# A hybrid decoder block on one core: mean square from token-major x on ScalarE, the scan phases' low part on ScalarE, the scores' scale in the rotation tables, and the last quarter of the scan taken last in the GLU

## Chip, core and metric

One core of a Trainium2 chip. The metric is the time of one execution on the device in microseconds (us), as the median of several runs. Inputs and weights lie in HBM in float32.

## What is computed

The reference is one decoder layer on 256 tokens of width 1024. Cut to what matters here:

```python
h = rms_norm(x, norm_mix_g)                  # x * rsqrt(mean(x*x) + 1e-6) * g
q, k, v, u, g = split(h @ w_in)              # 1024, 1024, 1024, 512, 2048 columns
q, k = rotary(q), rotary(k)                  # cos and sin tables by position
o_a = softmax(causal(q @ k.T * 128**-0.5)) @ v   # 8 heads of 128; one block of 256 tokens
o_b = s5_branch(u, ...)                      # complex diagonal scan, then gelu, then a GLU:
                                             #   hgl = gelu(y) @ w_glu; val * sigmoid(gate)
x = x + (sigmoid(g_a) * o_a + sigmoid(g_b) * o_b) @ w_out
x = x + square(relu(rms_norm(x, norm_mlp_g) @ w_up)) @ w_down
out = rms_norm(x, norm_final_g)
```

In the scan each of the 2048 states turns by an angle per step; the kernel needs the cosine and sine of (angle x position) for 16 tiles of 128 states.

## The kernel before, in words

**Products in three passes.** Each float32 product is made of three matmuls on rounded halves: weight high x input high, weight high x input low, weight low x input high (`mm3`, and `tok_mm` with the roles changed, L266 to L268). The halves come from `split` (L83, L84): ScalarE (ACT) casts the raw tile to its high half `hi_*`, VectorE (DVE) subtracts to get the low half `lo_*`. The names `hi_v`, `lo_v`, `raw_v` stand for the weights of v, and so on for q, k, g (first gate), gb (second gate), glu, wo, up and dn. Raw weights come in tiles of 512 KB over the SP queue (L70) into five buffers; four buffers each hold the high and the low halves.

**Order.** The engines' orders are not written by hand. A scheduler with a timing model places every instruction; `tc.high_priority` moves some forward, and the string `ORDER` gives the sequence of the parts of the first half: V (two chunks of v), P and C (small operations that prepare the scan), T (angle tables), Q (a quarter of the scan), K (q and k of a pair of heads), G, S, A (gate, scores and output of a pair of heads), B (second gate), X (a change of the ACT table set), Y (gelu). Each engine then runs its own list strictly in order; all loads named here go through SP's queue in its order.

**The parts that the change touches.**
- The first matmuls, u_acc (L180), run while x arrives in transposed form (xT, four pieces). From the same pieces ACT squares (sq, L185 and L187), DVE adds the squares up (L188), and PE sums over channels with matmuls against ones into ms (L205). DVE makes rsm of it (L208); POOL and DVE compute its reciprocal root in `rsqrt` (L192 to L200, the multiplications on POOL); rs_half is half of it (L213), rs_ps (L216) turns it into a row for all partitions.
- v runs in eight units of 12 matmuls of 512 columns, units 0 to 3 for the first chunk; unit n needs raw_v_n, hi_v and lo_v.
- `tables(m)` makes four angle tables per call: ACT multiplies positions by the high part of the angle (L515, tile q), DVE takes off whole turns (L516, L517) and adds positions times the low part (L519, one call for each of four tiles, tile tha). ACT then takes absolute values and sines (cs, sn).
- `prepare` makes the small coefficients s (L376 to L388, 128x16 each), then the tiles Bs on DVE and POOL (L454, L462), which PE transposes into the tile bt (L470) and ACT copies to W2.
- `attn_head` takes row maxima of the scores, multiplies them by minus the scale (L315), and gives the scale to the two Exp calls.
- After the first half `gelu` makes the four quarters of the scan's output into yhl, and the GLU's four column blocks q run over k = 0 to 3, each followed by a merge with the gates.

Of the kernel before, what the change touches and what calls it, by code (L numbers as in the profile page):

```python
# [16 lines left out]
P = 128  # L17
D = 1024
# [27 lines left out]
         "B0 G3 S3 X1 Y0 A3 B1")  # L46


def build(ctx, tc, dr, out):
# [14 lines left out]
    def att_bank(name):  # L64
        return bank("att", 2, name)
# [72 lines left out]
    early = {0: w_load(dr["w_in"][0], "v00")}  # L138
    cst = keep.tile([P, 896], F32, name="cst")
# [3 lines left out]
    ones = keep.tile([P, 1], F32, name="ones")  # L143
    V.memset(ones, 1.0)
# [13 lines left out]
    sq = p1.tile([P, KD, T], F32, tag="yhl", name="sq")  # L158
# [25 lines left out]
    for i, xk in enumerate((x0, xT[:, 1, :])):  # L184
        S.activation(sq[:, i, :], xk, AF.Square)  # L185
    for c in range(1, 4):
        S.activation(sq[:, 2 * c : 2 * c + 2, :], xT[:, 2 * c : 2 * c + 2, :], AF.Square)  # L187
        V.tensor_add(sq[:, 0:2, :], sq[:, 0:2, :], sq[:, 2 * c : 2 * c + 2, :])  # L188
# [13 lines left out]
    ms = att_bank("ms")  # L202
    for h in range(2):
        for i in range(2):
            PE.matmul(ms[:, 0, h : h + 1], sq[:, i, h * P : (h + 1) * P], ones,  # L205
                      start=(i == 0), stop=(i == 1))
    rsm = p1.tile([P, 6], F32, name="rsm")
    V.tensor_scalar(rsm[:, 0:2], ms[:, 0, 0:2], 1.0 / D, EPS, op0=ALU.mult, op1=ALU.add)  # L208
# [25 lines left out]
    V.tensor_mul(rcos, cos_c, rs)  # L234
    V.tensor_mul(rsin, sin_c, rs)
# [34 lines left out]
    def flat(x):  # L270
        return x.rearrange("p a b -> p (a b)")
# [29 lines left out]
    scale = P ** -0.5  # L301
    mixA = p1.tile([P, KD, T], F32, name="mixA")

    def attn_head(q, k, j):
        s = att_bank("s").rearrange("p a b -> p (a b)")
        PE.matmul(s[:, 0:128], q[:, j, 0:128], k[:, j, 0:128], start=True, stop=False,
                  skip_group_check=True)
        PE.matmul(s[:, 0:128], ident_b, tri_b, start=False, stop=True, skip_group_check=True)
        PE.matmul(s[:, 128:384], q[:, j, 128:256], k[:, j, :], start=True, stop=False,
                  skip_group_check=True)  # L310
        PE.matmul(s[:, 256:384], ident_b, tri_b, start=False, stop=True, skip_group_check=True)
        st = p1.tile([P, 6], F32, tag="st", bufs=2, name="st")
        V.tensor_reduce(st[:, 0:1], s[:, 0:128], axis=mybir.AxisListType.X, op=ALU.max)
        V.tensor_reduce(st[:, 1:2], s[:, 128:384], axis=mybir.AxisListType.X, op=ALU.max)
        V.tensor_scalar(st[:, 0:2], st[:, 0:2], -scale, None, op0=ALU.mult)  # L315
        pr = p1.tile([P, 384], F32, tag="pr", bufs=2, name="pr")
        act(pr[:, 0:128], s[:, 0:128], AF.Exp, bias=st[:, 0:1], scale=scale,
                     accum_out=st[:, 2:3])
        act(pr[:, 128:384], s[:, 128:384], AF.Exp, bias=st[:, 1:2], scale=scale,
                     accum_out=st[:, 3:4])  # L320
        V.reciprocal(st[:, 4:6], st[:, 2:4])
        S.activation(pr[:, 0:128], pr[:, 0:128], AF.Copy, scale=st[:, 4:5])
        S.activation(pr[:, 128:384], pr[:, 128:384], AF.Copy, scale=st[:, 5:6])
        return pr
# [276 lines left out]
    for step in ORDER.split():  # L601
# [24 lines left out]
        elif part == "Y":  # L626
            gelu()
# [16 lines left out]
    for q in range(4):  # L644
        acc = wide_banks(f"glu{q}") if q % 2 else [flat(mm_bank(f"glu{q}{h}")) for h in range(2)]
        for kk_ in range(2):
            wh, wl = w_unit(dr["w_glu"][2 * q + kk_], f"glu{q}{kk_}")
            for k2 in range(2):
                k, w = 2 * kk_ + k2, slice(k2 * 512, (k2 + 1) * 512)
                for hf in range(2):  # L650
                    tok_mm(acc[hf], wh[:, w], wl[:, w], yhl[0][:, 0:4], yhl[0][:, 4:8], k, hf,
                           k == 0, k == 3)
# [12 lines left out]
        split(mxh[:, two, :], mxl[:, two, :], mixA[:, two, :])  # L665
    ph1.__exit__(None, None, None)
# [213 lines left out]
```

## Time and profile before

| | |
|---|---|
| median of 3 runs | 404.85 us (404.71 to 405.25) |
| the profiled execution, its own time | 405.1 us |
| its span, first to last instruction | 403.2 us |
| PE busy / DVE busy / ACT busy | 98% / 73% / 56% |
| mean granted TensorE clock | 0.995 |
| DMA | 71.57 MB, mean 178 GB/s |

How to read it: all times below are us from the first instruction of the profiled execution. A row of the timeline has the start, the duration, the engine, the line of the program, the operation, output and input tiles with their shape, and a count where like instructions follow each other; in brackets is the time that the engine had stood idle before, and what ended it. Durations of neighbours on one engine overlap a little, so what an operation adds to its queue is the distance from start to start. Matmuls overlap most: a matmul of 256 columns shows 0.28 us and the next one starts 0.12 us later.

### The profile page before, as it was taken

Reading aid. Unit: us, or ns where it says so; the run is one execution under the profiler, and the core shown is the slowest. Engines: PE = TensorE matmul, PEld = TensorE weight load, DVE = VectorE, ACT = ScalarE, POOL = GpSimd, SP = SyncE. Lnnn points to the kernel's source line nnn. Section 1 sums busy time; section 2 is a strip of 40 time slices with the busy share of each in tenths; the row PEclk is TensorE's granted clock in tenths of the full one; section 3 lists DMA queues with packets and bytes.
Section 4 is the critical chain, followed back from the end, with each engine's and each line's share of the span. In section 5 each row is a group of like instructions: output and inputs, shape, how many; then the busy total and the mean of one; then the engine's idle time right before and its main releaser. Section 6 shows DMA issues by size and latency. Waiting matters only on the chain.

```text
span 403.2 us, 6862 instructions
## 1 busy us (share of the span) xinstructions
PE 394.3 (98%) x2635; PEld 355.2 (88%) x2635; DVE 292.8 (73%) x520; ACT 225.9 (56%) x360; POOL 30.3 (8%) x39
## 2 busy tenths in 40 slices
PE   8999999999999999999999999999999999999993
PEld 5988898989899787888889999999999888889983
DVE  5999999999999994769748665656565443564425
ACT  6767977655276557945647645464546334353323
POOL 4151492000000000000000000000000000000000
PEclk9999999999999999999999999999999999999998
DMA  8994843354516252456486465554555565555202
GB/s 228 401 337 149 246 154 102 111 202 151 192 56 208 84 195 102 158 159 206 161 308 209 152 215 191 176 194 172 191 178 193 172 205 169 199 192 178 101 0 104
DMA packets 23199, 71.57 MB, mean 178 GB/s; under 512 B 2944, under 2 KB 5248, under 8 KB 23168
## 3 DMA queue, kind: packets, MB, share of 16 engines
q1 hardware_dynamic: 20144, 68.92, 50.6%
q10 hardware_dynamic: 3024, 2.23, 1.9%
q8 instruction: 20, 0.33, 0.3%
q14 instruction: 11, 0.09, 0.1%
HBM read 69.18 MB, written 1.05 MB: 174 GB/s over the span
## 4 chain that ended last, share of the span: by engine, by line
PE 84%; DVE 5%; DMA 4%; ACT 2%; POOL 2%; issue 1%; ACTq 1%; SPq 0%; DVEq 0%
PE up L89 8%; PE up L90 8%; PE up L88 8%; PE dn L735 6%; PE dn L734 6%; PE dn L733 6%; PE k L88 2%; PE k L89 2%; PE k L90 2%; PE gb L268 2%; PE gb L266 2%; PE gb L267 2%; PE glu L268 2%; PE glu L266 2%; PE dnq L733 2%; PE dnq L735 2%
## 5 line engine op out<-in xcount | busy, mean ns | idle before, releaser
L89 PE MATMUL up<-x2l,hi_up 128*128 128x256 f32 x256 | 72.5, 284 | 0.0
L90 PE MATMUL up<-x2h,lo_up 128*128 128x256 f32 x256 | 72.3, 283 | 0.0
L88 PE MATMUL up<-x2h,hi_up 128*128 128x256 f32 x256 | 71.8, 283 | 0.0
L84 DVE TENSOR_TENSOR lo_dn<-raw_dn,hi_dn 128x1024 fp32r<-128x1024 f32 x32 | 39.2, 1225 | 44.0 <-ACT hi_dn L83 44.0
L83 ACT CAST hi_dn<-raw_dn 128x1024 fp32r<-128x1024 f32 x32 | 33.5, 1048 | 51.6 <-PE dn L735 25.8
L84 DVE TENSOR_TENSOR lo_up<-raw_up,hi_up 128x1024 fp32r<-128x1024 f32 x32 | 38.8, 1223 | 27.7 <-ACT hi_up L83 27.7
L83 ACT CAST hi_up<-raw_up 128x1024 fp32r<-128x1024 f32 x32 | 33.3, 1046 | 39.2 <-PE up L89 18.5
L89 PEld LDWEIGHTS up<-x2l,hi_up 128*128 128x128 f32 x256 | 49.1, 192 | 0.2 <-DVE x2l L694 0.2
L90 PEld LDWEIGHTS up<-x2h,lo_up 128*128 128x128 f32 x256 | 49.1, 192 | 0.0
L88 PEld LDWEIGHTS up<-x2h,hi_up 128*128 128x128 f32 x256 | 48.9, 192 | 0.1
L734 PE MATMUL dn<-lo_dn,hh 128*128 128x512 f32 x96 | 38.0, 395 | 0.0
L735 PE MATMUL dn<-hi_dn,hl 128*128 128x512 f32 x96 | 38.0, 395 | 0.0
L733 PE MATMUL dn<-hi_dn,hh 128*128 128x512 f32 x96 | 37.9, 395 | 0.0
L735 PEld LDWEIGHTS dn<-hi_dn,hl 128*128 128x128 f32 x96 | 18.0, 188 | 4.2
L733 PEld LDWEIGHTS dn<-hi_dn,hh 128*128 128x128 f32 x96 | 18.0, 188 | 3.8
L734 PEld LDWEIGHTS dn<-lo_dn,hh 128*128 128x128 f32 x96 | 18.0, 188 | 3.7
L89 PE MATMUL g<-xgl,hi_g 128*128 128x256 f32 x64 | 18.8, 294 | 0.0
L88 PE MATMUL k<-xgh,hi_k 128*128 128x256 f32 x64 | 18.4, 287 | 0.0
L90 PE MATMUL q<-xgh,lo_q 128*128 128x256 f32 x64 | 18.3, 286 | 0.0
L90 PE MATMUL g<-xgh,lo_g 128*128 128x256 f32 x64 | 18.3, 286 | 0.0
L90 PE MATMUL k<-xgh,lo_k 128*128 128x256 f32 x64 | 18.3, 286 | 0.0
L89 PE MATMUL q<-xgl,hi_q 128*128 128x256 f32 x64 | 18.3, 285 | 0.0
(267 smaller groups left out, 1046.9 us busy)
## 6 DMA issues: line engine op xcount, KB each, us to landing
raw_up<-w_up SPq DMA_DIRECT2D x32, 512.0 KB, 3.4
raw_dn<-w_down SPq DMA_DIRECT2D x32, 512.0 KB, 3.3
raw_v<-w_in SPq DMA_DIRECT2D x8, 512.0 KB, 6.0
raw_q<-w_in SPq DMA_DIRECT2D x8, 512.0 KB, 3.8
raw_k<-w_in SPq DMA_DIRECT2D x8, 512.0 KB, 3.2
raw_g<-w_in SPq DMA_DIRECT2D x8, 512.0 KB, 4.2
raw_gb<-w_in SPq DMA_DIRECT2D x8, 512.0 KB, 3.8
raw_glu<-w_glu SPq DMA_DIRECT2D x8, 512.0 KB, 3.2
```

The costliest lines, as they stand in the source:

```text
L83: ins = S.copy(hi, x).ins
L84: V.tensor_sub(lo, x, hi.bitcast(F32))
L88: PE.matmul(o, wh, xh, start=first, stop=False, **kw)
L89: PE.matmul(o, wh, xl, start=False, stop=False, **kw)
L90: PE.matmul(o, wl, xh, start=False, stop=last, **kw)
L266: PE.matmul(acc, xh[:, k, rows], wh, start=first, stop=False)
L267: PE.matmul(acc, xh[:, k, rows], wl, start=False, stop=False)
L268: PE.matmul(acc, xl[:, k, rows], wh, start=False, stop=last)
L733: PE.matmul(acc, xh, wh[:, w], start=(k == 0), stop=False, skip_group_check=True)
L734: PE.matmul(acc, xh, wl[:, w], start=False, stop=False, skip_group_check=True)
L735: PE.matmul(acc, xl, wh[:, w], start=False, stop=(k == 31), skip_group_check=True)
```

## The change

1. **Mean square.** x is loaded a second time, token-major, as one tile xtok of 1 MB, over SP directly behind the first tile of v's weights. Two ACT Squares of 1024 columns with an accumulated sum give ss; the squares of xT, the three DVE adds, ones and the ms matmuls are gone.
2. **Angle tables.** The four DVE operations of a call at L519 become four more ACT multiplications into a tile ulo and one DVE addition of 512 columns.
3. **Scale.** The rotation tables rcos and rsin carry the factor 128^-0.25 each, so scores come out scaled; the row maxima are negated where they are taken, and L315 is gone.
4. **GLU.** gelu is called for quarters 0 to 2 first. For q = 0 and 1 the GLU runs k = 0 to 2 of both, then comes gelu of quarter 3, the attention output of the last pair of heads (A3, taken out of `ORDER`), then k = 3 and the merge of each. q = 2 and 3 run as before.

```diff
-         "B0 G3 S3 X1 Y0 A3 B1")
+         "B0 G3 S3 X1 Y0 B1")
...
     early = {0: w_load(dr["w_in"][0], "v00")}
+    xtok = p1.tile([P, 2, D], F32, tag="yhl", name="xtok")
+    nc.sync.dma_start(xtok, dr["x"].rearrange("(h p) d -> p h d", p=P))
     cst = keep.tile([P, 896], F32, name="cst")
...
-    for i, xk in enumerate((x0, xT[:, 1, :])):
-        S.activation(sq[:, i, :], xk, AF.Square)
-    for c in range(1, 4):
-        S.activation(sq[:, 2 * c : 2 * c + 2, :], xT[:, 2 * c : 2 * c + 2, :], AF.Square)
-        V.tensor_add(sq[:, 0:2, :], sq[:, 0:2, :], sq[:, 2 * c : 2 * c + 2, :])
+    ss = p1.tile([P, 2], F32, name="ss")
+    for h in range(2):
+        S.activation(xtok[:, h, :], xtok[:, h, :], AF.Square, accum_out=ss[:, h : h + 1])
...
-    ms = att_bank("ms")
-    for h in range(2):
-        for i in range(2):
-            PE.matmul(ms[:, 0, h : h + 1], sq[:, i, h * P : (h + 1) * P], ones,
-                      start=(i == 0), stop=(i == 1))
     rsm = p1.tile([P, 6], F32, name="rsm")
-    V.tensor_scalar(rsm[:, 0:2], ms[:, 0, 0:2], 1.0 / D, EPS, op0=ALU.mult, op1=ALU.add)
+    V.tensor_scalar(rsm[:, 0:2], ss, 1.0 / D, EPS, op0=ALU.mult, op1=ALU.add)
...
-    V.tensor_mul(rcos, cos_c, rs)
-    V.tensor_mul(rsin, sin_c, rs)
+    V.scalar_tensor_tensor(rcos, cos_c, P ** -0.25, rs, op0=ALU.mult, op1=ALU.mult)
+    V.scalar_tensor_tensor(rsin, sin_c, P ** -0.25, rs, op0=ALU.mult, op1=ALU.mult)
...
-        V.tensor_reduce(st[:, 0:1], s[:, 0:128], axis=mybir.AxisListType.X, op=ALU.max)
-        V.tensor_scalar(st[:, 0:2], st[:, 0:2], -scale, None, op0=ALU.mult)
+        V.tensor_reduce(st[:, 0:1], s[:, 0:128], axis=mybir.AxisListType.X, op=ALU.max,
+                        negate=True)
-        act(pr[:, 0:128], s[:, 0:128], AF.Exp, bias=st[:, 0:1], scale=scale,
+        act(pr[:, 0:128], s[:, 0:128], AF.Exp, bias=st[:, 0:1],
...
+        ulo = rot("ulo")
         for q in range(4):
             S.activation(uhi[:, q, :], tpos, AF.Copy, scale=hi[:, 4 * m + q : 4 * m + q + 1])
+            S.activation(ulo[:, q, :], tpos, AF.Copy, scale=nlo[:, 4 * m + q : 4 * m + q + 1])
...
-        for q in range(4):
-            V.scalar_tensor_tensor(ang[:, q, :], tpos, nlo[:, 4 * m + q : 4 * m + q + 1],
-                                   ang[:, q, :], op0=ALU.mult, op1=ALU.add)
+        V.tensor_add(ang, ang, ulo)
...
+    first = [(q, glu_banks(q), glu_weights(q)) for q in range(2)]
+    for q, acc, ws in first:
+        glu_part(acc, ws, range(3))
+    gelu([3])
+    with tc.high_priority(ATT_PRIO):
+        attn_out(3, prs.pop(3), tha.pop(3))
+    for q, acc, ws in first:
+        glu_part(acc, ws, [3])
+        merge(q, acc)
+    for q in (2, 3):
+        acc = glu_banks(q)
+        glu_part(acc, glu_weights(q), range(4))
+        merge(q, acc)
```

`glu_part` holds the old inner loop for the given k, `merge` the old rest of the loop over q.

The change moves instructions at three places that the prediction speaks of. The rows are each engine's own order; the number behind a name is a buffer's.

The SP queue from the first tile of v's weights on, before:

```order
L70 DMA raw_v_87<-w_in 128x1024
L140 DMA cst<-cst 128x896
L70 DMA raw_v_328<-w_in 128x1024
L70 DMA raw_v_346<-w_in 128x1024
L70 DMA raw_v_364<-w_in 128x1024
```

and now:

```order
L70 DMA raw_v_87<-w_in 128x1024
L140 DMA xtok<-x 128x2x1024
L142 DMA cst<-cst 128x896
L70 DMA raw_v_317<-w_in 128x1024
L70 DMA raw_v_335<-w_in 128x1024
```

One transfer of twice a weight tile's size stands ahead of cst and of every later tile of v.

ACT in the first units of v (hi_v_312, 330, 348, 366, 388 are units 0 to 4), before:

```order
L83 CAST hi_v_312<-raw_v_87 128x1024
L83 CAST hi_v_330<-raw_v_328 128x1024
L83 CAST hi_v_348<-raw_v_346 128x1024
L83 CAST hi_v_366<-raw_v_364 128x1024
L83 CAST hi_v_388<-raw_v_386 128x1024
L515 ACTIVATE q<-cst,s_536 128x128 x8
```

and now (hi_v_301, 319, 337, 355 are units 0 to 3; q and ulo are table tiles):

```order
L83 CAST hi_v_301<-raw_v_87 128x1024
L186 ACTIVATE xtok,ss<-xtok 128x1024 x2
L83 CAST hi_v_319<-raw_v_317 128x1024
L509 ACTIVATE q<-cst,s_525 128x128 x6
L510 ACTIVATE ulo<-cst,s_527 128x128 x4
L509 ACTIVATE q<-cst,s_525 128x128 x2
L83 CAST hi_v_337<-raw_v_335 128x1024
L83 CAST hi_v_355<-raw_v_353 128x1024
```

Two Squares stand ahead of unit 1's cast, and twelve table operations ahead of unit 2's.

DVE between the low halves of v's units (lo_v_331, 349, 367, 389 are units 1 to 4), before:

```order
L84 TENSOR_TENSOR lo_v_331<-raw_v_328,hi_v_330 128x1024
...
L84 TENSOR_TENSOR lo_v_349<-raw_v_346,hi_v_348 128x1024
...
L84 TENSOR_TENSOR lo_v_367<-raw_v_364,hi_v_366 128x1024
...
L208 TENSOR_SCALAR rsm<-ms 128x2
...
L84 TENSOR_TENSOR lo_v_389<-raw_v_386,hi_v_388 128x1024
...
L213 TENSOR_SCALAR rs_half<-rsm 128x2
```

and now (lo_v_320 and 338 are units 1 and 2):

```order
L201 TENSOR_SCALAR rsm<-ss 128x2
...
L84 TENSOR_TENSOR lo_v_320<-raw_v_317,hi_v_319 128x1024
...
L206 TENSOR_SCALAR rs_half<-rsm 128x2
...
L513 TENSOR_TENSOR tha<-tha,ulo 128x512
...
L511 TENSOR_SCALAR tha<-q 128x512
...
L512 SCALAR_TENSOR_TENSOR tha<-tha,q 128x512
...
L84 TENSOR_TENSOR lo_v_338<-raw_v_335,hi_v_337 128x1024
```

rs_half, which needs POOL's result, and a piece of the first two tables stand between units 1 and 2; before, three more units went ahead of it.

## Rows read from the trace of the kernel before

**Rows 1.** The page: busy time, share and instructions of each engine; the granted TensorE clock in 40 slices, in tenths; and the chain that ended last, by engine.

```profile
PE 394.3 (98%) x2635; PEld 355.2 (88%) x2635; DVE 292.8 (73%) x520; ACT 225.9 (56%) x360; POOL 30.3 (8%) x39
...
PEclk9999999999999999999999999999999999999998
...
PE 84%; DVE 5%; DMA 4%; ACT 2%; POOL 2%; issue 1%; ACTq 1%; SPq 0%; DVEq 0%
```

**Rows 2.** The table by stretches: length, busy time and count of instructions for PE, weight loads, DVE, ACT and POOL, then the granted clock, the DMA engines' share and GB/s.

```profile
10.00:20.00 10.00, 10.00 (x85) 10.00 (x85) 9.37 (x22) 8.09 (x14) 1.75 (x2) 1.00 1.03 403
20.00:32.00 12.00, 12.00 (x55) 9.96 (x56) 11.33 (x59) 8.19 (x17) 7.23 (x15) 1.00 0.82 306
32.00:45.00 13.00, 13.00 (x70) 11.20 (x69) 13.00 (x35) 9.82 (x16) 0.00 (x0) 1.00 0.61 192
45.00:70.00 25.00, 24.08 (x208) 22.61 (x206) 24.12 (x42) 19.80 (x34) 16.60 (x13) 1.00 0.48 154
```

**Rows 3.** What PE waited for: us in total, times, longest.

```profile
PE bt L470 <- POOL Bs L454: 0.6, 1, 0.6
...
PE s L306 <- DVE k L298: 0.3, 1, 0.3
```

**Rows 4.** PE's timeline at these two waits.

```profile
47.63 0.28 PE L88 MATMUL q<-xgh,hi_q 128*128 128x256 f32 x1
48.48 0.98 PE L470 MATMUL bt<-cst,Bs 128*128 128x128 f32 x7 [0.58 <-POOL Bs L454]
...
65.09 0.28 PE L90 MATMUL g<-xgh,lo_g 128*128 128x256 f32 x1
65.72 0.46 PE L306 MATMUL s<-k,q 128*128 128x128 f32 x2 [0.34 <-DVE k L298]
```

**Rows 5.** PE's timeline at the first matmul of the GLU.

```profile
166.60 0.48 PE L266 MATMUL glu<-hi_glu,yhl 128*128 128x512 f32 x1
```

**Rows 6.** PE's timeline: ms, the first and the last v matmul, and the first row after them.

```profile
19.04 0.95 PE L205 MATMUL ms<-ones,sq 128*128 128x1 f32 x8
19.85 0.47 PE L266 MATMUL v<-hi_v,xgh 128*128 128x512 f32 x1
...
42.25 0.39 PE L268 MATMUL v<-hi_v,xgl 128*128 128x512 f32 x1
42.48 0.28 PE L90 MATMUL q<-xgh,lo_q 128*128 128x256 f32 x1
```

**Rows 7.** ACT's timeline: the first Square of the mean square.

```profile
3.97 0.40 ACT L185 ACTIVATE sq<-xg 128x256 f32<-128x256 f32 x1
```

**Rows 8.** PE's timeline in the u phase: four matmuls below and four at the full clock.

```profile
8.89 1.05 PE L180 MATMUL u_acc<-xgl,hi_u 128*128 128x256 f32 x4
...
10.39 0.64 PE L180 MATMUL u_acc<-xgh,hi_u 128*128 128x256 f32 x4
```

**Rows 9.** DVE's timeline: an addition of the mean square, ten small operations of the preparation, a low half of v, a table operation, and rs_half.

```profile
14.67 0.68 DVE L188 TENSOR_TENSOR sq<-sq 128x512 f32<-128x512 f32 x1
...
24.56 0.97 DVE L388 SCALAR_TENSOR_TENSOR s<-s,s 128x16 f32<-128x16 f32 x10
25.45 1.21 DVE L84 TENSOR_TENSOR lo_v<-raw_v,hi_v 128x1024 fp32r<-128x1024 f32 x1
...
26.84 0.43 DVE L516 TENSOR_SCALAR tha<-q 128x512 f32<-128x512 f32 x1
27.94 0.17 DVE L213 TENSOR_SCALAR rs_half<-rsm 128x2 f32<-128x2 f32 x1 [0.67 <-POOL rsm L200]
```

**Rows 10.** ACT's timeline: the casts of v's units 1 to 3, eight table operations and the cast behind them, and a cast of q.

```profile
17.64 1.05 ACT L83 CAST hi_v<-raw_v 128x1024 fp32r<-128x1024 f32 x1 [1.35 <-DMA raw_v<-w_in]
18.92 1.05 ACT L83 CAST hi_v<-raw_v 128x1024 fp32r<-128x1024 f32 x1 [0.23 <-DMA raw_v<-w_in]
20.18 1.05 ACT L83 CAST hi_v<-raw_v 128x1024 fp32r<-128x1024 f32 x1 [0.22 <-DMA raw_v<-w_in]
...
24.27 2.46 ACT L515 ACTIVATE q<-cst,s 128x128 f32<-128x128 f32 x8 [0.32 <-DVE s L415]
26.63 1.04 ACT L83 CAST hi_v<-raw_v 128x1024 fp32r<-128x1024 f32 x1
...
39.57 1.05 ACT L83 CAST hi_q<-raw_q 128x1024 fp32r<-128x1024 f32 x1 [2.26 <-DVE s L383]
```

**Rows 11.** POOL's timeline: the two casts from cst, the first operation of the rsqrt chain, and its longest.

```profile
16.32 0.41 POOL L257 CAST ident_b<-cst 128x128 bf16<-128x128 f32 x1 [11.06 <-DMA cst<-cst]
16.68 1.39 POOL L259 CAST tri_b<-cst 128x128 bf16<-128x128 f32 x1
23.22 0.30 POOL L195 TENSOR_SCALAR rsm<-rsm 128x2 f32<-128x2 f32 x1 [5.15 <-DVE s L388]
...
25.69 1.03 POOL L200 TENSOR_TENSOR rsm<-rsm 128x2 f32<-128x2 f32 x1
```

**Rows 12.** ACT's timeline at the second norm of the kernel: two Squares with accumulation.

```profile
216.67 1.06 ACT L697 ACTIVATE sq<-x2t 128x1024 f32<-128x1024 f32 x1
...
217.84 1.06 ACT L697 ACTIVATE sq<-x2t 128x1024 f32<-128x1024 f32 x1
```

**Rows 13.** Groups of instructions by line and shape: busy us and mean ns of one, then idle time before.

```profile
L519 DVE SCALAR_TENSOR_TENSOR tha<-cst,s,tha 128x128 f32<-128x128 f32 x16 | 5.1, 365 | 0.0
```

**Rows 14.** POOL's timeline at the last step of Bs.

```profile
45.16 5.60 POOL L454 TENSOR_SCALAR Bs<-ab 64x256 f32<-64x256 f32 x4 [13.19 <-DVE s L383]
```

More of the change, by code (lines that the diff above doesn't have):

```diff
@@ L142, in build @@
     ident, tri = cst[:, 640:768], cst[:, 768:896]
-    ones = keep.tile([P, 1], F32, name="ones")
-    V.memset(ones, 1.0)
     half_pi = keep.tile([P, 1], F32, name="half_pi")
@@ L157, in build @@
     xgl = keep.tile([P, KD, T], F32R, tag="xl", name="xgl")
-    sq = p1.tile([P, KD, T], F32, tag="yhl", name="sq")
     u_acc = ps.tile([P, 2, 2, T], F32, tag="x", name="u_acc")
@@ L299, in rope @@
         return o
-    scale = P ** -0.5
     mixA = p1.tile([P, KD, T], F32, name="mixA")
@@ L312, in attn_head @@
         st = p1.tile([P, 6], F32, tag="st", bufs=2, name="st")
-        V.tensor_reduce(st[:, 0:1], s[:, 0:128], axis=mybir.AxisListType.X, op=ALU.max)
-        V.tensor_reduce(st[:, 1:2], s[:, 128:384], axis=mybir.AxisListType.X, op=ALU.max)
-        V.tensor_scalar(st[:, 0:2], st[:, 0:2], -scale, None, op0=ALU.mult)
+        V.tensor_reduce(st[:, 0:1], s[:, 0:128], axis=mybir.AxisListType.X, op=ALU.max,
+                        negate=True)
+        V.tensor_reduce(st[:, 1:2], s[:, 128:384], axis=mybir.AxisListType.X, op=ALU.max,
+                        negate=True)
         pr = p1.tile([P, 384], F32, tag="pr", bufs=2, name="pr")
-        act(pr[:, 0:128], s[:, 0:128], AF.Exp, bias=st[:, 0:1], scale=scale,
+        act(pr[:, 0:128], s[:, 0:128], AF.Exp, bias=st[:, 0:1],
                      accum_out=st[:, 2:3])
-        act(pr[:, 128:384], s[:, 128:384], AF.Exp, bias=st[:, 1:2], scale=scale,
+        act(pr[:, 128:384], s[:, 128:384], AF.Exp, bias=st[:, 1:2],
                      accum_out=st[:, 3:4])
@@ L589, in build, with gelu @@
     yhl = []
-    def gelu():
-        yhl.append(p1.tile([P, KD, T], F32R, tag="yhl", name="yhl"))
+    def gelu(ms):
+        if not yhl:
+            yhl.append(p1.tile([P, KD, T], F32R, tag="yhl", name="yhl"))
         yflat = yT.rearrange("p m e j -> p m (e j)")
-        for m in range(4):
+        for m in ms:
             act(yflat[:, m, :], yflat[:, m, :], AF.Gelu_apprx_tanh)
@@ L626, in build @@
         elif part == "Y":
-            gelu()
+            gelu(range(3))
         elif part == "Q":
@@ L642, in wide_banks, with glu_weights, glu_banks, glu_part @@
         return [flat(b[:, h]) for h in range(2)]
[L644 to L652, printed above, removed]
+    def glu_weights(q):
+        return [w_unit(dr["w_glu"][2 * q + kk_], f"glu{q}{kk_}") for kk_ in range(2)]
+    def glu_banks(q):
+        return wide_banks(f"glu{q}") if q % 2 else [flat(mm_bank(f"glu{q}{h}")) for h in range(2)]
+    def glu_part(acc, ws, ks):
+        for k in ks:
+            w = slice(k % 2 * 512, (k % 2 + 1) * 512)
+            for hf in range(2):
+                tok_mm(acc[hf], ws[k // 2][0][:, w], ws[k // 2][1][:, w],
+                       yhl[0][:, 0:4], yhl[0][:, 4:8], k, hf, k == 0, k == 3)
+    def merge(q, acc):
         tp = att_bank(f"mt{q}")
```

## The prediction

> **What bounds the kernel now.** I read the page's totals first, then a table by stage, then what TensorE (PE) waited for, then single stretches of each engine. PE is busy for 98% of the span, its clock is granted in full in nearly every slice, and 84% of the chain that ended last is PE [rows 1]. By stage it is full from 10 to 45 us, and falls short by 0.9 us between 45 and 70 us [rows 2]. So nothing is to be gained behind a busy PE: time comes only from matmuls that disappear or from waits of PE, and is lost only where PE begins to wait. Beside two waits in the first 6 us PE waited for two things, 0.6 us for the tile Bs and 0.3 us for a rotated k [rows 3]. From start to start they are larger: the bt transposes come 0.85 us after the q matmul before them, the first scores matmul 0.63 us after a g matmul, where 0.12 us is usual: 0.73 and 0.51 us lost [rows 4]. In the GLU stage the first glu matmul starts with no idle time noted [rows 5].
>
> The profiled execution took 405.1 us, its span 403.2 us. The sum is made against 405.1; the median of the runs is 404.85, so 0.25 us come off at the end. Under 0.2%, or 0.8 us, a measurement can't be told from no change.
>
> **The mean square, at its old place.** The ms matmuls go: 0.8 us of PE, from 19.04 to 19.85 us [rows 6]. On ACT five Squares go; two early ones of 0.4 us [rows 7] stand ahead of the casts that PE needs at 5 us, so the u matmuls may end up to 0.6 us sooner; I take 0.3, since transfers bind there too. Three adds of 0.6 us go on DVE [rows 9]. The v matmuls could thus start at 18.7 us in place of 19.85. What these 1.1 us are worth depends on the weights being there.
>
> **What comes in their place on SP.** The 1 MB transfer xtok stands ahead of cst and of raw_v_1 to raw_v_7. Three hi_v casts in a row were released by their DMA, 1.28 and 1.26 us apart, so 512 KB take 1.27 us [rows 10]; the DMA share between 10 and 20 us is 1.03, so there is no room beside it [rows 2]. 1 MB takes 2.55 us. cst landed at 16.3 us [rows 11] and its 448 KB take 1.1, so raw_v00 landed at 15.2: xtok lands at 17.7, cst at 18.85, raw_v_1 at 17.64 + 2.55 = 20.2, raw_v_2 at 21.4.
>
> **ACT.** The two Squares with accumulation are 1.17 us each from start to start where the program has such a pair [rows 12], hence 17.7 to 20.0 us, while ACT would wait for raw_v_1 anyway. hi_v_1 is cast from 20.2 to 21.2. Then, by the new order, 12 table activations stand ahead of hi_v_2: eight took until the next cast 0.295 us each [rows 10], so 3.5 us. hi_v_2 is cast from 24.7 to 25.7; that cast began at 18.92 before.
>
> **POOL and DVE.** The rsqrt chain on POOL stands behind its two casts of cst, which end 1.75 us after cst lands [rows 11]: it starts at 20.7 us. It took 4.7 us, from 23.22 to rs_half's start at 27.94 [rows 9, 11], with one multiplication of 1.03 us that lay under the subtraction lo_v at 25.45; an operation of the chain starts 0.3 us after the one before, so without this it is 3.9 us. The new lo_v_1 (about 21.6 to 22.8) lies on the chain too, so it ends between 24.6 and 25.4 us. I take 25.0. The Trainium skill ("SBUF — State Buffer", Who interferes with whom) says that a DVE instruction with two SBUF inputs blocks a GpSimd instruction that reads SBUF until it is done; by that rule the later end and a sum 0.4 us above mine are right, and the 1.03 us row agrees with it.
>
> In the new order rs_half, which waits for POOL, stands ahead of lo_v_2; before, it stood behind lo_v_4. Between the two lie 2.25 us: rs_half and seven small operations at 0.09, two operations of 512 columns at 0.6 (as the add there) and one at 0.4 [rows 9]. lo_v_2 therefore starts at 25.0 + 0.1 + 2.2 = 27.3 and ends 1.2 us later, at **T = 28.5**. Bounds: 27.0, if only its cast counts (25.7 + 1.2), and 29.0, with the later end of POOL.
>
> **PE at that place.** 96 v matmuls took 22.6 us with rs_ps among them, 0.23 each [rows 6]. v00's twelve run from 18.7 to 21.4. Then PE waits 1 us for lo_v_1, runs unit 1 and rs_ps to 25.5, two hi matmuls of unit 2 at 25.7, and waits over 2 us for lo_v_2. What was gained ahead is gone. At T, 26 of the 96 are done; the other 70 take 16.1 us, so v ends at 44.6 us, against 42.48 [rows 6]: **+2.1 us** (bounds +0.6 and +2.6).
>
> **The tables.** Sixteen DVE operations (5.1 us busy, about 0.27 each as they follow each other) become sixteen ACT operations (4.7 us) and four additions (2.4 us) [rows 9, 10, 13]: DVE gains 1.9 us, ACT loses 4.7. PE sees this only through Bs and through casts. POOL waited 13.19 us for a small DVE operation ahead of Bs [rows 14], and DVE gets there with less ahead of it; I expect the waits of 0.73 and 0.51 us to go, -1.24 us. In their place come casts that are late on ACT, which was busy 18.0 of the 25 us between 20 and 45 us [rows 2] and gets 3.5 us of tables there: hi_q_8 and the copy of the transposed W2, about 0.4 us each. The trace shows neither of these two waits: the lower bound is zero, the upper the 2.26 us for which a hi_q cast stood still on ACT [rows 10]; 0.8 is nearer the lower, since all that PE lost in that stage before was 0.9 us [rows 2]. Net **-0.4 us** (-1.24 to +1).
>
> **Scale and GLU.** Eight DVE operations as small as rs_half's go, one per head; PE waited there for k, not for them: 0. In the GLU the last quarter of gelu moves behind 36 matmuls of q=0 and 1, which cover 36 x 0.23 = 8.3 us. PE did not wait there before [rows 5], so 0; with the cover gone it would wait for three operations of 256 columns, 1.2 us at the Square's 0.4 [rows 7].
>
> Sum: 405.1 + 2.1 - 0.4 = 406.8, on the median's scale **406.5 us**.
>
> **The rivals.**
> A: not slower. lo_v_2 follows its cast (T = 27.0, because POOL ends by 23.5 or its stretch on DVE is shorter), PE loses 0.6 us there, and the two old waits go with no new ones: 404.85 + 0.6 - 1.24 = 404.2. For it: both old waits hang on DVE work that this change cuts. Against: rs_half is in DVE's queue ahead of lo_v_2, and POOL starts only behind cst. It decides at T = 28.4 without new waits (28.4 + 16.1 - 42.48 - 1.24 = 0.8).
> B: ACT becomes what PE waits for from 25 to 60 us. Its DMAs, tables, copies of v and casts go in one order; if two casts that PE needs are late by 1 us each in place of my 0.4, and one more by 0.3, that is +1.5 us: 408.0. For it: 21.5 of 25 us busy. Against: PE's store of cast weights is four units deep.
> C: PE's clock falls in the pause before lo_v_2. The longest loss after 10 us in the trace is 0.73 us, and the granted clock stayed at 1.00 [rows 2, 4]. At 1.2 GHz four matmuls of 256 columns take 0.85 us from start to start, at 2.4 GHz 0.48 [rows 8], 0.09 more each; 22 such matmuls, about as many as ran so at the start of the u phase, cost 2.0 us: 408.5. The Trainium skill ("TensorE: Matmul & The Clock Gate", HAM oscillation) tells of a kernel whose waits for DMA dropped the clock again and again; no run here shows that.
>
> **How the numbers follow.** Forecast 0.45, A 0.30, B 0.20, C 0.05. A splits into 0.12 faster and 0.18 the same; of the forecast's own spread (T from 27.5 to 29, new waits 0 to 1.2 us: 404.9 to 407.4) 0.05 lies within 0.8 us of before. So faster 0.12, the same 0.23, slower 0.65. The range 403.8 to 408.6 reaches through A, B and C and leaves out their fringes.
>
> **What would show it.** Right: no ms; hi_v_1's cast at 20.2, hi_v_2's at 24.7 us; PE idle about 1 us before the first lo_v_1 matmul and over 2 us before the first lo_v_2 matmul; v's last matmul at 44 to 45 us; no wait for Bs; glu without a wait. Wrong: raw_v_1 landing before 19 us, lo_v_2 ending before 27.0, or PE losing over 1 us between 45 and 200 us.

## The result, and the profile after

The changed kernel took **407.79 us** (median; 405.75 to 410.03), the kernel before on the same chip 404.89 us (404.16 to 405.25): ratio 1.0075, 95% interval 1.0049 to 1.0101. The profiled execution of after took 410.03 us with a span of 408.2 and a mean granted clock of 0.986; that is the top of its range. The forecast was 406.5 us, slower, by TensorE (PE) waiting for v's weights. That happened; the sizes of its terms are another matter.

The page of after: busy time of each engine, the granted clock in 40 slices, and the chain that ended last, against [rows 1].

```profile
PE 395.0 (97%) x2627; PEld 353.9 (87%) x2627; DVE 288.0 (71%) x496; ACT 231.8 (57%) x375; POOL 34.9 (9%) x39
...
PEclk9987999999999999999999999999999999999997
...
PE 87%; DMA 5%; DVE 4%; POOL 1%; issue 1%; ACT 1%; SPq 1%; DVEq 0%; ACTq 0%
```

The table by stretches, against [rows 2], with the same columns.

```profile
10.00:20.00 10.00, 10.00 (x78) 9.66 (x77) 8.73 (x34) 7.24 (x13) 0.55 (x2) 1.00 1.04 409
20.00:32.00 12.00, 7.74 (x28) 5.14 (x28) 10.64 (x54) 11.53 (x28) 4.58 (x13) 0.86 0.56 205
32.00:45.00 13.00, 13.00 (x52) 10.55 (x51) 11.30 (x22) 9.49 (x16) 10.53 (x3) 0.87 0.88 285
45.00:70.00 25.00, 25.00 (x204) 23.68 (x204) 22.05 (x34) 21.51 (x39) 14.49 (x13) 1.00 0.53 175
```

The loss is between 20 and 45 us. PE is busy for 7.74 of 12 us there where it had been full, then full for 13 us but with 52 matmuls where there had been 70. The second row from below says why: the granted clock is 0.87. Behind 45 us PE is full, and the 0.9 us that it lacked before are gone. What PE waited for, against [rows 3]:

```profile
PE v L260 <- DVE lo_v L84: 3.0, 2, 2.3
...
PE v L259 <- ACT hi_v L83: 0.7, 1, 0.7
PE rs_ps L209 <- POOL rsm L198: 0.5, 1, 0.5
```

PE's timeline from the first to the last v matmul, against [rows 6]. hi_v in 21.57 is unit 1; the two hi matmuls of 26.64 are unit 2.

```profile
17.99 0.40 PE L259 MATMUL v<-hi_v,xgh 128*128 128x512 f32 x1
...
21.57 0.73 PE L259 MATMUL v<-hi_v,xgh 128*128 128x512 f32 x2 [0.67 <-ACT hi_v L83]
23.08 0.50 PE L260 MATMUL v<-lo_v,xgh 128*128 128x512 f32 x1 [0.77 <-DVE lo_v L84]
...
26.17 0.71 PE L209 MATMUL rs_ps<-cst,rsm 128*128 128x128 f32 x4 [0.54 <-POOL rsm L198]
26.64 0.71 PE L259 MATMUL v<-hi_v,xgh 128*128 128x512 f32 x2
29.62 0.79 PE L260 MATMUL v<-lo_v,xgh 128*128 128x512 f32 x1 [2.28 <-DVE lo_v L84]
30.21 0.63 PE L261 MATMUL v<-hi_v,xgl 128*128 128x512 f32 x1
...
34.05 1.71 PE L259 MATMUL v<-hi_v,xgh 128*128 128x512 f32 x4
35.60 0.39 PE L260 MATMUL v<-lo_v,xgh 128*128 128x512 f32 x1
...
48.35 0.39 PE L261 MATMUL v<-hi_v,xgl 128*128 128x512 f32 x1
48.59 1.03 PE L463 MATMUL bt<-cst,Bs 128*128 128x128 f32 x8
```

Two things are to be seen. There are four waits, and the long one is that for the low half of unit 2. And behind it the matmuls come 0.43 us apart (30.21 to 34.05: nine in 3.84 us) until 35.60, from where they come 0.23 apart again: 14 matmuls in 5.98 us in place of 14 x 0.228 = 3.19, so **2.8 us are lost to a clock of 1.2 GHz** (some 0.1 of it follows any wait: 23.08 to 23.41 at the full clock). From start to start the four waits cost 0.82, 1.05, 0.71 and 2.52 us, 5.1 in all. With the clock that is nearly all of the 7.96 us by which v takes longer (30.36 us from its first to its last matmul, 22.40 before); it starts 1.86 us sooner, so it ends 6.10 later. The bt transposes follow the last v matmul by 0.24 us, without a wait, against [rows 4].

Why unit 2's low half is late: ACT, POOL and DVE, against [rows 9 to 11].

```profile
17.71 1.06 ACT L186 ACTIVATE xtok<-xtok 128x1024 f32<-128x1024 f32 x1 [1.43 <-DMA xtok<-x]
...
20.47 1.05 ACT L83 CAST hi_v<-raw_v 128x1024 fp32r<-128x1024 f32 x1 [0.57 <-DVE s L369]
21.43 1.86 ACT L509 ACTIVATE q<-cst,s 128x128 f32<-128x128 f32 x6
...
24.95 1.98 ACT L83 CAST hi_v<-raw_v 128x1024 fp32r<-128x1024 f32 x2
```

```profile
19.10 0.31 POOL L252 CAST tri_b<-cst 128x128 bf16<-128x128 f32 x1
20.58 0.27 POOL L193 TENSOR_SCALAR rsm<-rsm 128x2 f32<-128x2 f32 x1 [1.17 <-DVE s L408]
...
21.89 1.21 POOL L198 TENSOR_TENSOR rsm<-rsm 128x2 f32<-128x2 f32 x1
23.18 0.53 POOL L195 TENSOR_TENSOR rsm<-rsm 128x2 f32<-128x2 f32 x1
...
24.07 0.64 POOL L197 TENSOR_SCALAR rsm<-rsm 128x2 f32<-128x2 f32 x1
...
34.47 10.21 POOL L455 TENSOR_SCALAR Bs<-bpad 128x512 f32<-128x512 f32 x2 [8.36 <-DMA bpad<-bpad]
```

```profile
20.03 0.16 DVE L201 TENSOR_SCALAR rsm<-ss 128x2 f32<-128x2 f32 x1
...
21.81 1.21 DVE L84 TENSOR_TENSOR lo_v<-raw_v,hi_v 128x1024 fp32r<-128x1024 f32 x1
...
23.22 0.42 DVE L511 TENSOR_SCALAR tha<-q 128x512 f32<-128x512 f32 x1
...
23.93 0.68 DVE L512 SCALAR_TENSOR_TENSOR tha<-tha,q 128x512 f32<-128x512 f32 x1
...
26.15 0.17 DVE L206 TENSOR_SCALAR rs_half<-rsm 128x2 f32<-128x2 f32 x1 [1.35 <-POOL rsm L198]
...
28.35 1.22 DVE L84 TENSOR_TENSOR lo_v<-raw_v,hi_v 128x1024 fp32r<-128x1024 f32 x1
```

xtok lands at 17.7, unit 2's cast starts at 24.95, both as forecast within 0.3 us. DVE then stands for 1.35 us at rs_half, behind POOL's chain, with lo_v_2 queued behind it. POOL operations of 0.2 us take 1.21 us beside lo_v_1 (21.81 to 23.02), 0.53 beside the table operation at 23.22, which has one input, and 0.64 beside the one at 23.93, which has two. POOL's casts of cst end at 19.41; it then stands 1.17 us until DVE has made rsm (from 20.03 on), which needs the second Square of xtok. So the chain hangs on xtok and its Squares here, not on cst.

The GLU's first matmul starts without a wait, against [rows 5]:

```profile
171.91 0.40 PE L259 MATMUL glu<-hi_glu,yhl 128*128 128x512 f32 x1
```

A count by milestones, start times in us in one profiled execution each; e11 and e12 are runs of the section below:

| | last v matmul | first glu | first wo | last matmul | execution |
|---|---|---|---|---|---|
| before | 42.25 | 166.60 | 191.12 | 396.77 | 405.1 |
| after | 48.35 | 171.91 | 195.61 | 401.67 | 410.03 |
| e11, after again | 45.20 | 168.76 | 192.45 | 397.80 | 406.15 |
| e12, after with idle matmuls | 46.31 | 169.33 | 193.01 | 398.36 | 406.71 |

From the last v matmul to the last one of all, before took 354.5 us, after 353.3, e11 352.6, e12 352.05: **the part behind v became 1.2 to 2.5 us shorter**. In these traces all of the loss, and more, is ahead of the end of v.

### The profile page after: what moved, and what is told of

Read it like the earlier page. It is cut to its first block, busy times and chain, and to the rows that moved or that the text cites. A ratio compares the mean times of both kernels' runs of the same rounds, so it can differ in the third digit from the quotient of the medians.

```text
span 408.2 us, 6825 instructions
## 1 busy us (share of the span) xinstructions
PE 395.0 (97%) x2627; PEld 353.9 (87%) x2627; DVE 288.0 (71%) x496; ACT 231.8 (57%) x375; POOL 34.9 (9%) x39
## 3 DMA queue, kind: packets, MB, share of 16 engines
HBM read 70.22 MB, written 1.05 MB: 175 GB/s over the span
## 4 chain that ended last, share of the span: by engine, by line
PE 87%; DMA 5%; DVE 4%; POOL 1%; issue 1%; ACT 1%; SPq 1%; DVEq 0%; ACTq 0%
PE up L89 8%; PE up L90 8%; PE up L88 7%; PE dn L749 5%; PE dn L748 5%; PE dn L747 5%; DMA x2t<-x 2%; PE g L88 2%; PE k L90 2%; PE q L89 2%; PE g L89 2%; PE k L88 2%; PE q L88 2%; PE g L90 2%; PE k L89 2%; PE q L90 2%
## 5 line engine op out<-in xcount | busy, mean ns | idle before, releaser
L88 PE MATMUL g<-xgh,hi_g 128*128 128x256 f32 x64 | 18.8, 294 | 0.0
L88 PE MATMUL q<-xgh,hi_q 128*128 128x256 f32 x64 | 18.3, 287 | 0.0
```

The lines of the kernel that those rows point to most:

```text
L88: PE.matmul(o, wh, xh, start=first, stop=False, **kw)
```

## Experiments

Theory: xtok ahead of v's weights delays unit 2, through POOL's chain, rs_half and lo_v_2; the falling clock comes on top. Rivals: another part of the change (the tables on ACT, the GLU's order) costs the time; the clock is only a symptom of one profiled execution.

### Which part

**e2: part 1 alone**, on the kernel before.

```diff
+    nc.sync.dma_start(xtok, dr["x"].rearrange("(h p) d -> p h d", p=P))
...
+        S.activation(xtok[:, h, :], xtok[:, h, :], AF.Square, accum_out=ss[:, h : h + 1])
...
-            PE.matmul(ms[:, 0, h : h + 1], sq[:, i, h * P : (h + 1) * P], ones,
```

> The kernel before with the new mean square alone (xtok, two Squares with accumulation); tables, scale and GLU as before. Theory: eight table operations instead of twelve ahead of hi_v_2's cast, rs_half still ahead of lo_v_2, so lo_v_2 ends at 28.5 to 29.5 us, v at 44.5 us or at 46 to 48.5 us where the clock falls, and 406.5 to 408.5 us in the median with runs 2 us or more apart. Rival (tables on ACT): below 405.5 us, PE waits less than 1 us before lo_v_2.

Measured: 407.56 us, ratio 1.0065 (1.0047 to 1.0082). The whole change has 1.0075, so part 1 alone is enough for a loss of nearly that size. PE's timeline of e2:

```profile
22.68 0.73 PE L259 MATMUL v<-hi_v,xgh 128*128 128x512 f32 x2 [0.30 <-ACT hi_v L83]
23.94 0.51 PE L260 MATMUL v<-lo_v,xgh 128*128 128x512 f32 x1 [0.53 <-DVE lo_v L84]
...
28.98 0.50 PE L260 MATMUL v<-lo_v,xgh 128*128 128x512 f32 x1 [1.55 <-DVE lo_v L84]
29.32 0.40 PE L261 MATMUL v<-hi_v,xgl 128*128 128x512 f32 x1
29.55 0.39 PE L260 MATMUL v<-lo_v,xgh 128*128 128x512 f32 x1
```

Pauses for the same halves, and behind the last one matmuls 0.23 us apart: here the clock did not fall.

**e8: part 4 alone** (the GLU's order).

```diff
-         "B0 G3 S3 X1 Y0 A3 B1")
+         "B0 G3 S3 X1 Y0 B1")
...
+        glu_part(acc, ws, range(3))
+    gelu([3])
```

> The kernel before with the GLU's new order alone. Theory (no wait of PE there before, fewer changes between kinds of matmuls at 0.09 us each): 404.3 to 404.9 us, no wait in the GLU. Rival (the transposes of the last heads' probabilities stand in PE's order ahead of a GLU matmul and wait for ACT, as in the kernel without xtok, where PE waited 5.8 us there): 407 to 411 us with one wait of 3 us or more for pr.

Measured: 405.06 us, ratio 1.0002 (0.999 to 1.0015). Part 4 costs and brings nothing that can be told, as forecast.

**e10: part 2 alone** (the tables' low part on ACT), **e7: parts 2 and 3**, **e1: all but part 1**.

```diff
+            S.activation(ulo[:, q, :], tpos, AF.Copy, scale=nlo[:, 4 * m + q : 4 * m + q + 1])
...
-            V.scalar_tensor_tensor(ang[:, q, :], tpos, nlo[:, 4 * m + q : 4 * m + q + 1],
-                                   ang[:, q, :], op0=ALU.mult, op1=ALU.add)
+        V.tensor_add(ang, ang, ulo)
```

(e7 adds the P ** -0.25 lines and takes L315 out; e1 is after with the old squares, adds and ms matmuls put back.)

> The kernel before with the tables' low part on ACT alone. Theory (it is this part that moves the last pair's scores behind 160 us and lets the pt transposes wait for ACT, as in the kernel with tables and scale): 412 to 414.5 us, one wait of 5 to 6 us for pr. Rival (the scale's part does that): 403.8 to 405.5 us and no such wait.

> The kernel before with the tables on ACT and the scale in the rotation tables, without the second load of x and without the GLU's new order. Theory (these two parts move work off DVE, the wait for Bs goes and nothing else changes): 403.8 to 405.2 us. Rival (ACT's longer queue makes casts late, as in the kernel without xtok, where PE waited 1.7 us for a lo_v at 38 us): PE waits 1 to 2 us between 28 and 45 us, 405.5 to 407 us.

> The changed kernel with the mean square put back as before (squares of xT, three adds, ms matmuls, no xtok); tables, scale and GLU stay changed. Theory (the loss is the second load of x: late weights of v, then ACT, POOL and DVE ahead of lo_v_2, and the clock that falls in that pause): v ends at 42.5 us again, no pause of PE between 20 and 35 us, 404.0 to 405.0 us, spread of the runs below 1 us. Rival (the 16 table operations on ACT are the loss, since they stand ahead of casts): casts of v or q come late, PE waits between 28 and 60 us, 406 to 408 us.

Measured: e10 416.93 us, 1.0304 (1.0279 to 1.0329); e7 413.61, 1.0221 (1.0197 to 1.0246); e1 412.80, 1.0206 (1.0181 to 1.0231). Without part 1 the rest of the change costs 8 to 12 us, in each of the three runs more than its own theory or rival allowed. PE and ACT of e10 ahead of the GLU:

```profile
170.65 1.09 PE L329 MATMUL pt<-cst,pr 128*128 128x128 f32 x3 [2.79 <-ACT pr L322]
176.26 0.47 PE L329 MATMUL pt<-cst,pr 128*128 128x128 f32 x1 [4.53 <-ACT pr L322]
```

```profile
171.46 1.28 ACT L101 ACT_TABLE_LOAD   x1
172.75 1.33 ACT L107 ACTIVATE yT<-yT 128x256 f32<-128x256 f32 x4
173.99 1.54 ACT L107 ACTIVATE thb<-gb,rs_half 128x256 f32<-128x256 f32 x4
...
175.78 0.43 ACT L322 ACTIVATE pr<-pr,st 128x128 f32<-128x128 f32 x1
```

The last scores matmuls are at 167.15 us (155.35 before; 165.0 and 165.5 in e1 and e7), so the last pair's pr reaches ACT when the table change, gelu and tanh stand ahead of it, and PE's pt transposes, ahead of the GLU in PE's order, wait for it: 7.3 us in all, 5.8 in e1 and in e7. Behind these waits the clock falls too (0.50 from 172 to 180 us in e10). The three kernels also wait 1.28 (e10), 1.99 (e7) and 1.73 us (e1) for a low half of v between 38 and 39 us, the wait that e7's rival named; in e1 its cast starts on ACT only at 35.87. In the complete change the last scores are at 156.98 us and there is neither wait. So **the parts do not add up**: with part 1 in place, the scheduler places the rest without these waits. Which rule of the scheduler turns it, the runs do not show. In the windows from 105 to 140 us DVE is busy for 35.0 of 35 us in e1, e7 and e10, 34.6 in before and 33.0 in after, which goes with late scores, but e6 below is full as well and waits 0.4 us there.

### What holds unit 2

**e3: the reciprocal root on DVE in place of POOL.**

```diff
-        rsqrt(G, rs_tok, rsm[:, 0:2], rsm[:, 4:6])
+        rsqrt(V, rs_tok, rsm[:, 0:2], rsm[:, 4:6])
```

> The changed kernel with the rsqrt chain on DVE instead of POOL (rsqrt called with the vector engine). Theory (POOL's chain, stretched under DVE's two-input operations, holds rs_half and with it lo_v_2): rs_half no longer waits 1.35 us, lo_v_2 ends at 27.0 to 28.2 us instead of 29.57, PE's pause before it is 1.3 us shorter, 406.0 to 407.0 us. Rival (the weights' landing and the twelve table operations alone set lo_v_2): it ends within 0.5 us of 29.57 and the time stays within 0.5 us of 407.8.

Measured: 408.46 us, 1.0082 (1.0064 to 1.0101). The first lo_v_2 matmul starts at 28.52 us, 1.1 earlier than in after, although the first Square of xtok started 0.95 us later (18.66), with clock 1.00 from 20 to 45 us; but rs_ps moved in PE's order to 36.35, the scan's input came later, and PE waited 1.1 us for its transfer at 52.42. POOL's chain is on the path, but the total gives the gain back and misses the theory's 406 to 407; beyond that 1.1 us the runs do not show where.

**e5: rs_half behind lo_v_4.**

```diff
-    V.tensor_scalar(rs_half, rs_tok, 0.5, None, op0=ALU.mult)
...
+                behind(V.tensor_scalar(rs_half, rs_tok, 0.5, None, op0=ALU.mult).ins,
+                       lo4, "rs_half behind lo_v_4")
```

> The changed kernel with one DVE instruction moved: rs_half, which waits for POOL's rsqrt chain, is tied behind lo_v_4; every other instruction of DVE, ACT and PE keeps its place. Theory (rs_half's wait of 1.35 us ahead of lo_v_2 is a part of PE's pause there): lo_v_2 ends at 28.1 to 28.4 us instead of 29.57, v's last matmul is 1.2 us earlier where the clock holds, the median is 0.8 to 1.5 us below 407.8. Rival (what is gained there is given back at Bs or at a cast of q, as in the kernel with rsqrt on DVE): lo_v_2 ends at the same 28.1 to 28.4, but the median stays within 0.4 us of 407.8 and PE waits for Bs or hi_q.

Measured: 407.38 us, 1.0049 (1.0029 to 1.0069). DVE no longer stands, and the wait moves to PE, at rs_ps, which needs the same chain:

```profile
27.93 1.03 PE L210 MATMUL rs_ps<-cst,rsm 128*128 128x128 f32 x4 [2.58 <-POOL rsm L200]
```

```profile
26.59 1.29 POOL L200 TENSOR_TENSOR rsm<-rsm 128x2 f32<-128x2 f32 x1
```

With DVE at two-input operations without a break, POOL's chain ended at 27.9 us, not 26.1. The median lies 0.4 us below that of after, not the theory's 0.8 to 1.5. rs_half's wait is thus a symptom: whichever engine reads the chain's result first stands.

**e9: rs_half and also rs_ps with what hangs on it behind unit 2.**

```diff
+            behind(mm, others, 'rs_ps behind unit 2')
...
+            if first == 0 and kk_ == 2:
+                rs_part([end])
```

> The changed kernel with both readers of POOL's rsqrt chain moved: rs_half tied behind lo_v_4 on DVE, and the rs_ps matmuls (with the copy and the products that hang on them) behind v's unit 2 on PE. Theory (the pause ahead of unit 2 is POOL's chain, stretched to 5.5 to 7.3 us under DVE's two-input operations, once through rs_half, once through rs_ps): lo_v_2 is ready at 28.0 to 28.4 us, PE waits for no POOL before it, one pause of 1.5 to 2 us is left that the cast and DVE's table work set, v's last matmul at 43.8 to 44.5 us where the clock holds, median 405.8 to 406.8 us. Rival (the gain is given back at Bs, whose transposes the new order puts ahead in PE's list): v's last matmul as early, but a wait of 1 us or more for Bs and a median of 407 or more.

Measured: 408.31 us, 1.0078 (1.0054 to 1.0102). No wait for POOL; lo_v_2 at 28.38 us. But waits of 0.91, 0.53, 0.64 and 1.09 us for v's halves remain, and the clock fell behind them (0.86 from 20 to 32 us). So POOL's chain is about 1 us of lo_v_2's delay (29.62 in after, with xtok's first Square 0.25 us later than here) and not all of it. The rest of unit 2's is not its weights' landing: raw_v_2 landed by 23.0 us, and its cast on ACT starts at 25.46, straight behind the table operations. The median missed the theory's 405.8 to 406.8, and the rival's wait for Bs did not come.

**e6: half of xtok.**

```diff
-    nc.sync.dma_start(xtok, dr["x"].rearrange("(h p) d -> p h d", p=P))
+    nc.sync.dma_start(xtok[:, 0, :], dr["x"][0:P, :])
```

> The changed kernel with half of xtok: 512 KB are loaded in place of 1 MB, and both Squares read that half (this leaves out the mean square of the second 128 tokens). Theory (each 512 KB ahead of v's weights costs 1.27 us of their landing, and the order of DVE and ACT around it): raw_v_1 lands at 18.9, PE's waits between 20 and 32 us fall from 4.3 us to 1.5 to 2.5, 405.0 to 406.5 us. Rival (the landing of the weights is not what counts, the Squares, tables and POOL's chain are): PE's waits there stay above 3.5 us and the time above 407.

Measured: 407.16 us, 1.0057 (1.0043 to 1.007), between theory and rival. From 20 to 32 us one pause of 0.23 us is left, the clock is 1.00, one wait of 0.99 us for a low half comes at 37.78 us, and v's last matmul is at 42.94 us, +0.7 in place of +3 or more. So half of the second load takes most of the delay in v away. But the scheduler changed the orders as well: here unit 2's cast (20.53 us) stands ahead of the table operations, and lo_v_2 (21.79) ahead of rs_half (24.80). What the bytes do by themselves and what the orders do, the runs do not separate. The total did not follow. From v's last matmul to the first glu it takes 126.4 us, where before took 124.35 and after 123.6; the last scores are late, at 160.99 us, as in e10, but PE's wait for pr is only 0.4 us, so the rest of this is not explained.

### The clock

**e11: the kernel after once more**, unchanged, for a second trace.

> The changed kernel itself once more, to read a second trace of it. If the clock falls in the pause ahead of lo_v_2 by chance only, this trace shows either a granted clock of 1.00 from 20 to 45 us, v's last matmul at 45.3 to 45.7 us and 406 to 407.5 us, or a fall again, v's last at 47 to 48.5 us and 408 to 410. If something else sets the scatter of its runs, the time goes another way than v's last matmul.

Measured: 406.15 us. PE's timeline:

```profile
22.00 0.73 PE L259 MATMUL v<-hi_v,xgh 128*128 128x512 f32 x2 [1.47 <-ACT hi_v L83]
...
23.95 0.63 PE L260 MATMUL v<-lo_v,xgh 128*128 128x512 f32 x1
...
29.16 0.50 PE L260 MATMUL v<-lo_v,xgh 128*128 128x512 f32 x1 [0.85 <-DVE lo_v L84]
29.50 0.39 PE L261 MATMUL v<-hi_v,xgl 128*128 128x512 f32 x1
```

The clock fell here too, but earlier, in unit 1; PE would have waited for lo_v_2 in any case, so the spell at 1.2 GHz only shortens that wait (0.85 in place of 2.28 us). v ends 3.15 us sooner than in the first trace and the execution is 3.9 us shorter. Neither branch of the expectation came as written: the clock fell, and v was early all the same. Between these two executions of one program the place of the spell makes most of the difference. It does not make all of the scatter: the mean granted clock of each execution is known, and in after 406.90 us goes with 0.990 and 409.07 with 0.995; the six of e3 have 0.996 to 0.998 and lie 1.9 us apart. What makes the rest is open.

**e4: twelve idle matmuls** in the pauses of units 1 and 2.

```diff
+            if first == 0 and kk_ in (1, 2):
+                idle = att_bank("idle").rearrange("p a b -> p (a b)")
+                for _ in range(4 * kk_):
+                    PE.matmul(idle, wh[:, 0:P], wh[:, 0:512], start=True, stop=True)
```

> The changed kernel with 4 and 8 more matmuls of 512 columns whose result nobody reads, on the high halves of v's units 1 and 2, in PE's pauses ahead of lo_v_2 (2.7 us of added PE work). Theory (the clock falls in these pauses, and 14 matmuls at 1.2 GHz behind them cost 2.8 us): the granted clock stays at 1.00 from 20 to 45 us, the median is 406.2 to 407.3 us and the runs lie within 1.5 us of each other. Rival (the clock is not a part of the median's loss): 407.8 us or up to 0.5 us more, with the same spread of over 3 us.

Measured: 407.41 us, 1.0056 (1.0038 to 1.0074); 406.19 to 408.09. Clock 1.00 from 20 to 45 us in the profile (406.73 us). The executions at 409 to 410 are gone, but the median lies just above the theory's 407.3, the runs 1.9 us apart in place of 1.5, and the interval overlaps that of after: not settled by this run.

**e12: eighteen idle matmuls**, in all three pauses, into a bank of the scan's.

```diff
+            if first == 0 and kk_ == 2:
+                fill(wh, 8)
...
+            if first == 0 and kk_ < 2:
+                fill(wh, (6, 4)[kk_])
```

> The kernel after, with idle matmuls of 512 columns in the three pauses of v: six on hi_v_0 behind unit 0, four on hi_v_1 behind unit 1, eight on hi_v_2 ahead of its low part (18 in all, 0.23 us each, 4.1 us of PE work that writes a bank nobody reads). The pauses before unit 1 and unit 2 were 0.7 to 1.5, 0.5 to 0.8 and 0.9 to 2.3 us in the two profiles of the kernel after. Theory (clock): the clock stays at full speed from 20 to 45 us, v's last matmul starts at 44.8 to 45.6 us, the runs lie within 2 us of each other, and the median is 406.0 to 407.0 us, so that the falling clock makes about 1 us of the median of 407.8. Rival (the fall is mostly hidden in the waits): the granted clock is full in these stretches too, but the median stays at 407.3 to 408.2 us. Third possibility: the idle matmuls run longer than the pauses and delay unit 1 or unit 2 by up to 1 us; then the table of PE's waits shows under 0.5 us of waits for hi_v and lo_v together and v ends after 45.6.

Measured: 406.45 us (405.90 to 407.31), 1.0037 (1.0023 to 1.0052). The table by stretches, and PE's waits:

```profile
20.00:32.00 12.00, 11.04 (x50) 8.47 (x49) 10.65 (x60) 11.33 (x28) 4.65 (x14) 1.00 0.54 192
32.00:45.00 13.00, 13.00 (x60) 10.80 (x59) 12.35 (x22) 12.30 (x22) 7.77 (x3) 1.00 0.95 331
```

```profile
PE v L260 <- DVE lo_v L84: 1.0, 2, 0.6
```

The theory's median and spread (1.4 us) are met; v's last matmul at 46.31 us is later than it said, not by the idle matmuls (PE still waits for both low halves) but because in this execution xtok's first Square started at 18.38 us, 0.67 later than in after, and lo_v_2 as much. With the clock held the median is 1.3 us lower; the intervals of e12 and after still touch (1.0049 to 1.0052). That the clock makes these 1.3 us is likely but not shown: e4 had a clock of 1.00 in its profile too, and its median is only 0.4 us below that of after.

## Why the prediction was right, and where it was not

**Right: the direction, the place and the chain.** The 1 MB on SP: xtok at 17.7 us (17.71 measured), hi_v_1's cast at 20.2 (20.47), hi_v_2's at 24.7 (24.95). The hit at 17.7 is closer than the runs are to each other: the first Square of xtok starts between 17.44 us (e5) and 18.66 (e3) in kernels with the same loads. The 2.2 us on DVE from rs_half to lo_v_2 came out as 2.20 (26.15 to 28.35). e2 and e6 show that part 1 and its load of x cause it, e6 with the orders that go with the load. No wait for Bs, none for the GLU, and part 4 at nothing (e8).

**Right by luck: the chain's start.** It was put at 20.7 us, behind POOL's two casts of cst. It came at 20.58, but these casts had ended at 19.41 (0.29 and 0.31 us each, where before had 0.41 and 1.39), and POOL stood 1.17 us for rsm on DVE, a wait that the working did not have.

**Mis-sized: POOL's chain.** The term was 4.3 us to rs_half, with one stretched operation and the end at 25.0, bounds 24.6 to 25.4. Measured: 5.57 us (20.58 to 26.15), in e11 about 5.2. Three operations were stretched (two in e11) and not one; without these 1.8 us the chain has the 3.8 us that the working had (3.9). The Trainium skill ("SBUF — State Buffer", Who interferes with whom) would have DVE's two-input operations block GpSimd's reads; the traces agree (0.2 us became 1.21 beside a 1.21 us lo_v). e5 goes the same way: with unbroken DVE work the chain's end moved from 26.1 to 27.9. The bound allowed for one hit, where every long DVE operation in the stretch can be one; one of the three in after (0.53 us at 23.18) stands beside an operation with one input. T was 29.57 us, against 28.5 forecast and 29.0 as its upper bound. The step from T to the end of v was right: T + 16.1 us gives 45.2 in e11 (T = 29.11), where the first matmul behind v starts at 45.43.

**Left out of the sum: the clock.** Rival C had 0.05, because a loss of 0.73 us had left the clock at 1.00 in before. The clock fell in both traces of after, at 1.2 GHz for 14 matmuls in one and nine in the other; the price was 2.8 us in the first and little in the second. Rival C's 2.0 us for a spell behind T was 0.8 short; what it lacked was that the same spell ahead of a wait is nearly free. In the median it makes up to about 1.3 us, if all of e12's gain is the clock's.

**Mis-sized the other way: behind v.** The term was -0.4: two old waits gone (-1.24), 0.8 of new waits for casts. The old waits went, the new ones did not come, and from v's last to the first wo matmul after is 0.4 us shorter still (147.26 against 148.87 us, less 1.24). Measured -1.2 to -2.5. That rest was not taken apart.

So the forecast of +1.7 agrees with the +1.6 that e12 measures with the clock held, but by luck, since two errors cancel: v's last matmul is 3.0 (e11) to 4.1 us (e12) later without a costly spell, against 2.1, and the part behind v gives back 1.9 to 2.5, against 0.4. The 1.3 us between e12 and after lead to 407.8.

**The rivals.** A (not slower) fell with T above its point of 28.4 us. B (ACT becomes the bound) did not come, though it is what happens without part 1: in e10 mainly through the scores' place (7.3 us), and in e10, e7 and e1 also through a late low half of v (1.28 to 1.99 us). That the parts depend on each other in this way was in no rival.

## What to carry to other kernels

A transfer put ahead of weights that a busy PE needs delays more than the weights: follow every chain that hangs on it, on each engine's own order (here Squares and table operations on ACT, small GpSimd operations, the low half on DVE), and count a stretch for every long DVE operation beside a GpSimd chain. Taking one chain out is not enough where the next stands close behind: e3 and e9 brought unit 2 forward by 1.1 and 1.2 us and the total not at all. Price several pauses of PE close together with a spell at half clock behind the last of them (2.8 us in after), and with next to nothing if a wait swallows it (e11). Where a scheduler places everything, parts of a change are not to be priced or tried one by one as if they added up: one alone cost 12 us, and the whole cost 3.

## What the runs showed of the hardware

- **When the clock falls.** In v's stretch it fell in after (pauses of 0.67, 0.77, 0.54, 2.28 us), e11 (1.47 and 0.53, already at 23.6 us) and e9 (0.91, 0.53, 0.64, 1.09), and in e5 (0.74, 0.72, 2.58); it did not fall in e2 (0.30, 0.53, 1.55), e3 (0.58, 1.12, 1.11) and e4 (1.52, 0.53). Neither the longest pause nor their sum divides these cases: 2.0 us in all sufficed in e11, 2.8 did not in e3. e4 had the same matmuls as e11 up to 26 us and the same two pauses to 0.05 us, and the clock fell in one and not in the other. The Trainium skill ("TensorE: Matmul & The Clock Gate", HAM oscillation) tells of waits for DMA that make it fall again and again; here the waits were for ACT, DVE and POOL, of 2.58 us at most, and in this stretch it fell once in each of these traces.
- **GpSimd under DVE.** The first two operations of Bs on 128x512 took 4.06 us together in e11, 3.69 in e12, and 10.21 in after, where three low halves of v (35.88, 38.23, 40.63 us) and small two-input products stand on DVE beside them. e11 has the same operations on DVE (35.41, 38.18, 40.59 us), so they alone do not explain the difference: there POOL was done by 37.98, and one product on DVE took 0.84 us (at 36.55) where its like take 0.42. PE waited for Bs in none of the three.
